# Two heads' attention worked as a pair, with query-key products alternating between the row halves of TensorE

## The chip, the cores and the metric

The kernel runs on one core of one Trainium2 chip. The core has a matrix engine (TensorE: PE in the profile, its weight loads PEld), a vector engine (VectorE, DVE), a scalar engine (ScalarE, ACT), GpSimd (POOL) and an engine that issues transfers (SyncE, SP). Each works off its own queue in order. TensorE writes to PSUM, from where VectorE and ScalarE fetch its results. The metric is the device time of one execution in microseconds, less being better.

## The reference

A two-layer encoder runs over two sequences that share their weights, one of 512 and one of 256 tokens, with a model width of 1024. The change is in the mixer of the first layer, which has eight attention heads of width 64 beside a short gated convolution:

```python
def window_conv_mixer(xn, pos, w_in, w_out, conv_w):
    z = xn @ w_in
    q, k, v, bg, cg, h = jnp.split(z, cuts, axis=-1)
    q = partial_rotary(heads(q), pos) * (HEAD_DIM ** -0.5)
    k = partial_rotary(heads(k), pos)
    ya = dilated_attention(q, k, heads(v)).reshape(B, S, A_WIDTH)
    yb = short_gated_conv(bg, cg, h, conv_w)
    return jnp.concatenate([ya, yb], axis=-1) @ w_out
```

`dilated_attention` runs three banded branches (window 128, 512 and 2048 with dilation 1, 4 and 16) and mixes them by the softmax of their log-sums. That equals one softmax over all keys in which each key's exponential is weighted by the number of branches that see it, and this is what the kernel computes. Behind the mixer come, in both layers, a cross-attention to 256 memory tokens and a SwiGLU; the second layer's mixer is an RWKV-7 recurrence.

## The kernel before

Activations lie with channels on partitions and tokens in columns, T = 768 columns for both sequences (`SEQS` cuts them at 512). A dense product is made from float32r pieces: each operand is cut into a high and a low part, and three matmuls (high by high, high by low, low by high) stand for one float32 product. `mms` (lines 342 to 344) does this for dense products: 8 blocks of 128 channels, for each block three matmuls with 512 columns and three with 256, 24 of each per output block of 128 channels. `products` (line 333) does the same for the attention.

In the first layer's mixer a pair p of heads shares one block of 128 channels: head 0 on partitions 0 to 63, head 1 on 64 to 127. There are four pairs. `keys(p)` and `values(p)` make q, k and v of a pair, `turned` transposes v, `conv(p)` makes the convolution's output of a block, `out(p)` adds the pair's share of the output product to the residual (line 755). `attend(p)` does the attention of a pair: for head 1 and then head 0, for each sequence, for each tile of 128 queries, it makes the three query-key products into a PSUM tile "sm" (a 64-row product: the contraction is over one head's 64 channels), adds the mask and takes the maximum (line 716, VectorE), exponentiates (718, ScalarE), weights by the count and sums (720), inverts the sum (722) and scales (723). The tile before it is then handed to `turn`: transposes by TensorE into another "sm" tile (693), a copy of the high part by ScalarE (695), the low part by VectorE (696), and after every second tile the products with v into `py` (line 333 again). Head 1's probabilities are multiplied with both heads' columns of v, and head 0's products then overwrite its half.

In PSUM "sm" has two buffers of 512 columns, "mm" for the dense products two of 768, `py` one. "e", the exponentials' tile, has three buffers. `bigs` holds the other work tiles.

The order of issue is set in two steps. `weave` interleaves generators: at each step it advances the one that is least far along relative to the number given with it. The order in which instructions are written becomes their priority. A planner then lays the instructions out on a simulated clock (the kernel asks for it with `schedule_with_timeline_sim=True`): an engine that is free takes the instruction of highest priority among those whose operands and buffers are ready. The resulting order of each engine is fixed, and on the chip each queue waits at its head. In the kernel before, the four pairs' attention is one generator of 52 steps, woven with one chain of dense work of 70 and the normalisation of the memory tokens of 32:

```python
weave((attends(), 52), (itertools.chain(*dense), 70), (mem_norm, 32, 12))
weave((part(out, 3), 4))
```

`dense` is the list of convolutions, keys, values and outputs in the order in which they are needed, with the memory's keys and values for the first cross-attention (`mem_kv`, `mem`) as its last members, some of them ahead of out(2). In the second layer, line 1179 (`inverse` in `mixer1_scan`) makes products with 64 rows whose loop alternates between the halves of the array; its operands are plain float32.

Of the kernel before, what the change touches and what calls it, by code (L numbers as in the profile page):

```python
# [9 lines left out]
F32 = mybir.dt.float32  # L10
# [27 lines left out]
class Net:  # L38
# [85 lines left out]
    def consts(self):  # L124
        nc, a = self.nc, self.a
        self.ident = self.cst.tile([128, 128], F32, name="ident")
        make_identity(nc, self.ident)
        self.ones = self.cst.tile([128, 128], F32, name="ones")
        nc.vector.memset(self.ones, 1.0)
        self.col = param_columns()  # L130
        n = sum(VECTORS.values())
        self.par = self.cst.tile([128, n], F32, name="par")
        nc.sync.dma_start(self.par, a["par"])
        self.mu = self.cst.tile([128, 2, 48], F32, name="mu")
        m = self.par[:, self.col["rw_mu"]:self.col["rw_mu"] + 48]
        nc.gpsimd.tensor_scalar(self.mu[:, 0], m, -1.0, 1.0, op0=OP.mult, op1=OP.add)
        nc.gpsimd.tensor_scalar(self.mu[:, 1], m, 0.5, None, op0=OP.mult)

        self.gmu = self.cst.tile([128, 2, 48], F32, name="gmu")
        c = self.col["norm_mix"] + KT  # L140
        nc.gpsimd.tensor_mul(self.gmu.rearrange("p a (i m) -> p (a i) m", m=KT), self.mu.rearrange("p a (i m) -> p (a i) m", m=KT),
                             self.par[:, c:c + KT].unsqueeze(1).to_broadcast([128, 12, KT]))
# [61 lines left out]
    def rstd(self, acc, spread=True):  # L204
# [4 lines left out]
        for t in range(n):  # L209
            for i, s in enumerate(acc):  # L210
                nc.tensor.matmul(ps[:, t:t + 1], lhsT=s[:, t * 128:(t + 1) * 128], rhs=self.ones[:, 0:1],  # L211
# [410 lines left out]
    def mixer0(self):  # L622
# [62 lines left out]
        def attend(p, o):  # L685
            q, k = o["q"], o["k"]
            py = self.pmm.tile([128, T], F32, name="py", bufs=1)

            def turn(e, pT, hs, s0, t, n):

                p2 = self.psm.tile([128, 4, 128], F32, name="sm")
                for i in range(n // 128):
                    nc.tensor.transpose(p2[:, i, :], e[:, i * 128:(i + 1) * 128], self.ident)
                hi, lo = cut(pT, slice(0, n // 128), slice(t % 2 * 128, t % 2 * 128 + 128))
                nc.scalar.copy(hi, p2[:, :n // 128])
                nc.vector.tensor_sub(lo, p2[:, :n // 128], hi.bitcast(F32))
                if t % 2:
                    c = s0 + t * 128 - 128

                    vs = slice(0, hs.stop)  # L700
                    self.products(py[vs, c:c + 256], [(cut(o["V"], s0 // 128 + i, vs), cut(pT, i)) for i in range(n // 128)])
            todo = None
            for h in (1, 0):
                hs = slice(64 * h, 64 * h + 64)
                for s0, s1 in SEQS:
                    n = s1 - s0
                    for t in range(n // 128):
                        if t % 2 == 0:
                            pT = [self.ph.tile([128, 4, 256], F32R, name="pT" + s, bufs=1) for s in "hl"]
                        off = 384 - 128 * t  # L710
                        ps = self.psm.tile([128, 512], F32, name="sm")
                        c = s0 + t * 128
                        self.products(ps[:, :n], [([a[hs, c:c + 128] for a in q], [a[hs, s0:s1] for a in k])])
                        e = self.at(512).big("e")
                        mx = self.tp.tile([128, 1], F32, name="mx0")
                        nc.vector.tensor_tensor_reduce(e[:, :n], ps[:, :n], self.mask[:, off:off + n], -1.0, 3e38,
                                                       OP.add, OP.min, mx)
                        nc.scalar.activation(e[:, :n], e[:, :n], AF.Exp, bias=mx, scale=-1.0)
                        den = self.tp.tile([128, 1], F32, name="den0")
                        nc.vector.tensor_tensor_reduce(e[:, :n], e[:, :n], self.cnt[:, off:off + n], 1.0, 0.0,  # L720
                                                       OP.mult, OP.add, den)
                        nc.vector.reciprocal(den, den)
                        nc.vector.tensor_scalar_mul(e[:, :n], e[:, :n], den)
                        if todo:
                            turn(*todo)
                        todo = e, pT, hs, s0, t, n
                        yield
            turn(*todo)
            o["ya"] = self.split(py, tag="y", bufs=6)
            yield  # L730

        def conv(p, o):
# [12 lines left out]
            o["yb"] = self.split(h, tag="y", bufs=6)  # L745
            yield

        def out(p, o):
            wa = self.wcols(w_out, p * 128, 1, 0, D)
            wb = self.wcols(w_out, 512 + p * 128, 1, 0, D)  # L750
            for m in range(KT):
# [4 lines left out]
                if m % 2:  # L756
# [6 lines left out]
        dense = [two(conv, 0), two(keys, 1), two(values, 1), two(conv, 1), two(keys, 2), part(out, 0), two(conv, 2),  # L763
                 two(values, 2), two(keys, 3), two(conv, 3), part(out, 1), two(values, 3), take(mem, 12), part(out, 2), mem]
# [5 lines left out]
        def attends():  # L770
            for p in range(4):
                turned(st[p])
                yield from attend(p, st[p])
        weave((attends(), 52), (itertools.chain(*dense), 70), (mem_norm, 32, 12))
# [267 lines left out]
    def mixer1_scan(self, L, rkv, zs, bvs, fill):  # L1042
# [33 lines left out]
        def prep(u, o):  # L1076
# [80 lines left out]
            for p, c in parts:  # L1157
                rk = self.tp.tile([128, 128], F32, name="rk")
# [459 lines left out]
```

## Time and profile before

| | us |
|---|---|
| median of three runs | 3124.48 |
| lowest, highest | 3120.39, 3129.13 |
| the profiled execution | 3129.72 |
| its span, first to last instruction | 3127.9 |
| TensorE busy in it | 2967.1 |
| VectorE busy in it | 1863.9 |

Times are compared by medians; durations and spans come from the one profiled execution. A row of the profile names the line, the engine, the operation, the tile written and those read ("sm<-qk"), the shape, and how often it stands (x3). For a matmul the shape is rows by output partitions of the array, then partitions by columns. A matmul's duration reaches from its start to its modelled end, and matmuls overlap in the pipeline. The first-layer attention lies between about 60 and 450 us; the mixer's last addition to the residual, by out(3), ends at about 485 us.

### The profile page before, as it was taken

Reading aid. Unit: us, or ns where it says so; the run is one execution under the profiler, and the core shown is the slowest. Engines: PE = TensorE matmul, PEld = TensorE weight load, DVE = VectorE, ACT = ScalarE, POOL = GpSimd, SP = SyncE. Lnnn points to the kernel's source line nnn. Section 1 sums busy time; section 2 is a strip of 40 time slices with the busy share of each in tenths; the row PEclk is TensorE's granted clock in tenths of the full one; section 3 lists DMA queues with packets and bytes.
Section 4 is the critical chain, followed back from the end, with each engine's and each line's share of the span. In section 5 each row is a group of like instructions: output and inputs, shape, how many; then the busy total and the mean of one; then the engine's idle time right before and its main releaser. Section 6 shows DMA issues by size and latency. Waiting matters only on the chain. (4 is left out here: it accounts for less than half of the span.)

```text
span 3127.9 us, 50086 instructions
## 1 busy us (share of the span) xinstructions
PE 2967.1 (95%) x19984; PEld 2465.7 (79%) x19984; DVE 1863.9 (60%) x3492; ACT 1223.7 (39%) x2241; POOL 608.6 (19%) x617
## 2 busy tenths in 40 slices
PE   7999999999999989889989999999999999999997
PEld 6888788888888867768767776666678888888886
DVE  8687547464354595376788777676636464334345
ACT  3232435332222375454546664554445232112112
POOL 3113004020000110122244223433335120000001
PEclk9999999999999999988979997999999999999998
DMA  3123332112355657644434552222352212212211
GB/s 116 48 68 115 105 118 85 58 54 68 119 192 193 218 173 261 203 155 144 142 104 146 165 158 75 71 71 66 117 166 79 71 41 68 68 54 68 68 55 54
DMA packets 349257, 344.15 MB, mean 110 GB/s; under 512 B 40928, under 2 KB 287840, under 8 KB 349024
## 3 DMA queue, kind: packets, MB, share of 16 engines
q1 hardware_dynamic: 349024, 340.96, 33.7%
q8 instruction: 157, 2.57, 0.3%
q14 instruction: 76, 0.62, 0.1%
HBM read 269.06 MB, written 71.83 MB: 109 GB/s over the span
## 5 line engine op out<-in xcount | busy, mean ns | idle before, releaser
L342 PE MATMUL mm<-xs,whi 128*128 128x512 f32 x2128 | 754.7, 356 | 32.0 <-ACT whi L274 11.8
L343 PE MATMUL mm<-xs,whi 128*128 128x512 f32 x2128 | 756.1, 355 | 3.1 <-DVE xs L237 2.2
L344 PE MATMUL mm<-xs,wlo 128*128 128x512 f32 x2128 | 750.4, 353 | 2.1 <-DVE wlo L275 2.1
L274 ACT CAST whi<-wraw 128x1024 fp32r<-128x1024 f32 (+1 forms) x246 | 256.3, 1044 | 789.1 <-PE mm L343 755.8
L342 PEld LDWEIGHTS mm<-xs,whi 128*128 128x128 f32 x2128 | 404.7, 190 | 95.6 <-ACT whi L274 12.4
L343 PEld LDWEIGHTS mm<-xs,whi 128*128 128x128 f32 x2128 | 404.6, 190 | 60.8 <-issue 3.3
L344 PEld LDWEIGHTS mm<-xs,wlo 128*128 128x128 f32 x2128 | 403.5, 190 | 60.7 <-DVE wlo L275 3.7
L275 DVE TENSOR_TENSOR wlo<-wraw,whi 128x1024 fp32r<-128x1024 f32 (+1 forms) x246 | 310.0, 1262 | 157.2 <-ACT whi L274 148.1
L201 POOL TENSOR_TENSOR acc<-acc,sq 128x768 f32<-128x768 f32 (+2 forms) x72 | 121.2, 1683 | 1417.3 <-ACT sq L198 1032.8
L343 PE MATMUL mm<-fb,thi 128*128 128x256 f32 (+1 forms) x720 | 236.3, 328 | 0.0
L342 PE MATMUL mm<-hid,whi 128*128 128x512 f32 (+1 forms) x528 | 186.5, 356 | 1.9 <-ACT hid L233 1.9
L343 PE MATMUL mm<-hid,whi 128*128 128x512 f32 (+1 forms) x528 | 187.8, 356 | 0.0
L344 PE MATMUL mm<-hid,wlo 128*128 128x512 f32 (+1 forms) x528 | 186.4, 354 | 0.0
L342 PE MATMUL mm<-fb,thi 128*128 128x256 f32 x528 | 170.3, 323 | 7.0 <-ACT thi L303 5.1
L303 ACT CAST thi<-traw 128x512 fp32r<-128x512 f32 (+1 forms) x202 | 122.6, 608 | 123.6 <-PE mm L343 72.0
L344 PE MATMUL mm<-fb,tlo 128*128 128x256 f32 x528 | 157.9, 301 | 10.2 <-DMA tlo<-low 5.2
L383 DVE SCALAR_TENSOR_TENSOR u<-mm,rstd 128x768 f32<-128x768 f32 (+1 forms) x44 | 38.4, 873 | 211.3 <-PE mm L344 211.3
L343 PEld LDWEIGHTS mm<-fb,thi 128*128 128x128 f32 x720 | 147.2, 204 | 5.1 <-issue 1.2
L403 DVE TENSOR_TENSOR x<-x,mm 128x512 f32<-128x512 f32 (+2 forms) x56 | 42.4, 762 | 175.3 <-PE mm L344 175.1
L1206 DVE TENSOR_TENSOR lt<-xr,lane 128x30 f32<-128x30 f32 (+4 forms) x360 | 130.4, 362 | 8.4
L342 PE MATMUL mm<-fa,thi 128*128 128x512 f32 (+1 forms) x304 | 132.5, 437 | 0.2 <-DVE fa L448 0.2
L1207 DVE TENSOR_TENSOR xr<-xr,lt 128x30 f32<-128x30 f32 (+4 forms) x360 | 124.7, 346 | 8.4
(366 smaller groups left out, 5906.2 us busy)
## 6 DMA issues: line engine op xcount, KB each, us to landing
wraw<-in_ffn_wgu_dram SPq DMA_DIRECT2D x44, 1024.0 KB, 4.9
tlo<-low SPq DMA_DIRECT2D x128, 256.0 KB, 3.2
low<-wlo SPq DMA_DIRECT2D x60, 512.0 KB, 3.1
wraw<-in_ffn_wdown_dram SPq DMA_DIRECT2D x23, 1024.0 KB, 4.9
traw<-in_ffn_wgu_dram SPq DMA_DIRECT2D x56, 256.0 KB, 3.8
wraw<-in_ab_w_in_dram SPq DMA_DIRECT2D x24, 512.0 KB, 3.6
wraw<-in_ca_wkv_dram SPq DMA_DIRECT2D x8, 1024.0 KB, 5.5
kvd<-kv SPq DMA_DIRECT2D x32, 256.0 KB, 2.0
```

Of the source, the lines that this page charges most:

```text
L201: nc.gpsimd.tensor_add(acc, acc, sq)
L274: nc.scalar.copy(hi[:, :, :m], raw[:, :, j:j + m])
L275: nc.vector.tensor_sub(lo[:, :, :m], raw[:, :, j:j + m], hi[:, :, :m].bitcast(F32))
L303: nc.scalar.copy(hi[:, :n], raw[:, :n])
L342: nc.tensor.matmul(ps[:, s0:s1], lhsT=wh, rhs=xh[:, s0:s1], start=start and k == 0, stop=False)
L343: nc.tensor.matmul(ps[:, s0:s1], lhsT=wh, rhs=xl[:, s0:s1], start=False, stop=False)
L344: nc.tensor.matmul(ps[:, s0:s1], lhsT=wl, rhs=xh[:, s0:s1], start=False, stop=stop and k == n - 1)
L383: nc.vector.scalar_tensor_tensor(u, pu, 0.5, rstd, op0=OP.mult, op1=OP.mult)
L403: self.nc.vector.tensor_add(self.x[m], self.x[m], ps)
L1206: nc.vector.tensor_mul(t, xr[:, m:, k:k + 1].to_broadcast([128, n, k]), ln[:, k:k + 1, 0:k].to_broadcast([128, n, k]))
L1207: nc.vector.tensor_add(xr[:, m:, 0:k], xr[:, m:, 0:k], t)
```

## The change

`attend` loops over sequences and query tiles once and treats both heads in each turn. The six query-key products of a pair of tiles are written so that heads alternate: pass one of head 0 and of head 1, pass two of both, pass three of both. Each head has its own "sm" tile, so both buffers are taken. Reductions and exponentials of both follow, and between them the transposes of the previous pair's tiles, first head 0's, then head 1's; the products with v of both heads follow head 1's transposes. Sum, inverse and scaling stand in a second step, the inverse for both heads in one instruction. The transposed probabilities need two sets of tiles.

The one chain of dense work becomes a list for each pair of heads, and each pair's attention is woven with its own list. The memory's keys and values stand at the end of the last list. "y", the tiles of split results that out(p) reads, goes from six buffers to four; `ones` shrinks to one column; `rk` of the second layer moves to another pool.

```diff
-        self.ones = self.cst.tile([128, 128], F32, name="ones")
+        self.ones = self.cst.tile([128, 1], F32, name="ones")
...
+            heads = [slice(0, 64), slice(64, 128)]
+            passes = ((0, 0), (0, 1), (1, 0))
-            def turn(e, pT, hs, s0, t, n):
+            def turn(h, es, pT, s0, t, n):
+                m = n // 128
                 p2 = self.psm.tile([128, 4, 128], F32, name="sm")
...
-                if t % 2:
+                if h and t % 2:
                     c = s0 + t * 128 - 128
-                    vs = slice(0, hs.stop)
-                    self.products(py[vs, c:c + 256], [(cut(o["V"], s0 // 128 + i, vs), cut(pT, i)) for i in range(n // 128)])
+                    for vs, pt in ((slice(0, 128), pT[1]), (slice(0, 64), pT[0])):
+                        self.products(py[vs, c:c + 256], [(cut(o["V"], s0 // 128 + i, vs), cut(pt, i)) for i in range(m)])
             todo = None
-            for h in (1, 0):
-                hs = slice(64 * h, 64 * h + 64)
-                for s0, s1 in SEQS:
-                    n = s1 - s0
-                    for t in range(n // 128):
-                        if t % 2 == 0:
-                            pT = [self.ph.tile([128, 4, 256], F32R, name="pT" + s, bufs=1) for s in "hl"]
-                        off = 384 - 128 * t
-                        ps = self.psm.tile([128, 512], F32, name="sm")
-                        c = s0 + t * 128
-                        self.products(ps[:, :n], [([a[hs, c:c + 128] for a in q], [a[hs, s0:s1] for a in k])])
...
-                        if todo:
-                            turn(*todo)
-                        todo = e, pT, hs, s0, t, n
-                        yield
-            turn(*todo)
-            o["ya"] = self.split(py, tag="y", bufs=6)
+            for s0, s1 in SEQS:
+                n = s1 - s0
+                for t in range(n // 128):
+                    if t % 2 == 0:
+                        pT = [[self.ph.tile([128, 4, 256], F32R, name=f"pT{h}" + s, bufs=1) for s in "hl"] for h in range(2)]
+                    off = 384 - 128 * t
+                    ps = [self.psm.tile([128, 512], F32, name="sm") for _ in heads]
+                    c = s0 + t * 128
+                    for j, (u, v) in enumerate(passes):
+                        for h, hs in enumerate(heads):
+                            nc.tensor.matmul(ps[h][:, :n], lhsT=q[u][hs, c:c + 128], rhs=k[v][hs, s0:s1], start=j == 0, stop=j == 2)
+                    es, mx = [], self.tp.tile([128, 2], F32, name="mx0")
+                    for h in range(2):
+                        e = self.at(512).big("e")
+                        es.append(e)
+                        nc.vector.tensor_tensor_reduce(e[:, :n], ps[h][:, :n], self.mask[:, off:off + n], -1.0, 3e38,
+                                                       OP.add, OP.min, mx[:, h:h + 1])
+                        nc.scalar.activation(e[:, :n], e[:, :n], AF.Exp, bias=mx[:, h:h + 1], scale=-1.0)
+                        if todo:
+                            turn(h, *todo)
+                    yield
+                    den = self.tp.tile([128, 2], F32, name="den0")
+                    for h, e in enumerate(es):
+                        nc.vector.tensor_tensor_reduce(e[:, :n], e[:, :n], self.cnt[:, off:off + n], 1.0, 0.0,
+                                                       OP.mult, OP.add, den[:, h:h + 1])
+                    nc.vector.reciprocal(den, den)
+                    for h, e in enumerate(es):
+                        nc.vector.tensor_scalar_mul(e[:, :n], e[:, :n], den[:, h:h + 1])
+                    todo = es, pT, s0, t, n
+                    yield
+            for h in range(2):
+                turn(h, *todo)
+            o["ya"] = self.split(py, tag="y", bufs=4)
...
-        dense = [two(conv, 0), two(keys, 1), two(values, 1), two(conv, 1), two(keys, 2), part(out, 0), two(conv, 2),
-                 two(values, 2), two(keys, 3), two(conv, 3), part(out, 1), two(values, 3), take(mem, 12), part(out, 2), mem]
+        dense = [[two(conv, 0), two(keys, 1), two(values, 1)],
+                 [two(keys, 2), part(out, 0), two(conv, 1), two(values, 2)],
+                 [two(keys, 3), part(out, 1), two(conv, 2), two(values, 3)],
+                 [part(out, 2), two(conv, 3), mem]]
...
-        def attends():
-            for p in range(4):
-                turned(st[p])
-                yield from attend(p, st[p])
-        weave((attends(), 52), (itertools.chain(*dense), 70), (mem_norm, 32, 12))
+        for p, ds in enumerate(dense):
+            turned(st[p])
+            weave((attend(p, st[p]), 13), (itertools.chain(*ds), 4 * len(ds)), *[(take(mem_norm, 5), 12, 3)] * (p in (1, 2)))
         weave((part(out, 3), 4))
...
-                rk = self.tp.tile([128, 128], F32, name="rk")
+                rk = ph.tile([128, 128], F32, name="rk", bufs=2)
```

## Rows read from the trace of the kernel before

**Rows 1.** The page: busy us (share) xinstructions; busy tenths in 40 slices.
```profile
PE 2967.1 (95%) x19984; PEld 2465.7 (79%) x19984; DVE 1863.9 (60%) x3492; ACT 1223.7 (39%) x2241; POOL 608.6 (19%) x617
...
PE   7999999999999989889989999999999999999997
```

**Rows 2.** Windows: length, busy PE, PEld, DVE, ACT, POOL, PEclk, DMA share, GB/s.
```profile
60.00:450.00 390.00, 389.19 (x2159) 322.89 (x2158) 269.69 (x518) 128.10 (x192) 51.29 (x35) 1.00 0.26 84
160.00:180.00 20.00, 20.00 (x105) 15.85 (x105) 19.96 (x36) 6.05 (x8) 7.19 (x6) 1.00 0.19 54
450.00:520.00 70.00, 69.97 (x400) 60.94 (x399) 39.87 (x52) 32.52 (x48) 25.66 (x12) 1.00 0.36 121
```

**Rows 3.** Waits of TensorE from 60 to 450 us: total us, times, longest.
```profile
PE mm L342 <- ACT xs L236: 0.5, 1, 0.5
PE sm L333 <- DVE mx L716: 0.3, 1, 0.3
```

**Rows 4.** Timeline of TensorE around a 512-key product group: start us, us, what.
```profile
162.54 0.29 PE L343 MATMUL mm<-xs,whi 128*128 128x256 f32 x1
162.66 0.28 PE L344 MATMUL mm<-xs,wlo 128*128 128x256 f32 x1
162.87 0.96 PE L333 MATMUL sm<-qk 64*128 64x512 f32 x3
163.76 0.51 PE L342 MATMUL mm<-xs,whi 128*128 128x512 f32 x1
164.11 0.40 PE L343 MATMUL mm<-xs,whi 128*128 128x512 f32 x1
164.34 0.40 PE L344 MATMUL mm<-xs,wlo 128*128 128x512 f32 x1
```

**Rows 5.** Timeline of TensorE around a 256-key product group.
```profile
96.92 0.60 PE L693 MATMUL sm<-ident,e 128*128 128x128 f32 x4
97.45 0.61 PE L333 MATMUL sm<-qk 64*128 64x256 f32 x3
98.00 0.39 PE L343 MATMUL mm<-xs,whi 128*128 128x256 f32 x1
98.22 0.28 PE L344 MATMUL mm<-xs,wlo 128*128 128x256 f32 x1
```

**Rows 6.** Timeline of TensorE: two groups in direct succession.
```profile
66.50 1.65 PE L333 MATMUL sm<-qk 64*128 64x512 f32 x6
```

**Rows 7.** Timeline of TensorE, second layer: line 1179, two visits.
```profile
1660.80 1.16 PE L1179 MATMUL g<-ar,bk 64*128 64x128 f32 x8
1661.88 0.50 PE L1026 MATMUL e<-blk,kksq 128*128 128x2 f32 x3
...
1734.44 1.16 PE L1179 MATMUL g<-ar,bk 64*128 64x128 f32 x16
1735.53 0.39 PE L344 MATMUL mm<-fb,tlo 128*128 128x256 f32 x1
```

**Rows 8.** Lines, 60 to 450 us: busy us, mean ns, idle before.
```profile
L275 DVE TENSOR_TENSOR wlo<-wraw,whi 128x1024 fp32r<-128x1024 f32 x40 | 51.7, 1294 | 14.7 <-ACT whi L274 9.8 <-PE sm L490 4.8
...
L333 PE MATMUL sm<-qk 64*128 64x512 f32 (+1 forms) x144 | 40.9, 389 | 0.3 <-DVE mx L716 0.3
...
L716 DVE CUSTOM_DVE_ANT_0 e<-sm,mask 128x512 f32<-128x512 f32 (+1 forms) x48 | 28.7, 599 | 20.7 <-PE sm L333 20.6
L696 DVE TENSOR_TENSOR pTl<-sm,pTh 128x512 fp32r<-128x512 f32 (+1 forms) x48 | 28.6, 598 | 29.4 <-ACT pTh L695 29.2
...
L693 PE MATMUL sm<-ident,e 128*128 128x128 f32 x160 | 25.4, 273 | 0.0
L695 ACT CAST pTh<-sm 128x512 fp32r<-128x512 f32 (+1 forms) x48 | 24.6, 514 | 89.5 <-PE sm L693 82.4 <-PE py L333 7.0
...
L722 DVE RECIPROCAL den<-den 128x1 f32<-128x1 f32 x48 | 7.7, 161 | 0.9
L486 ACT COPY kv<-mm 128x512 f32<-128x512 f32 x13 | 7.6, 585 | 1.7 <-PE mm L344 1.7
```

More of the change, by code (lines that the diff above doesn't have):

```diff
@@ L210, in rstd @@
             for i, s in enumerate(acc):
-                nc.tensor.matmul(ps[:, t:t + 1], lhsT=s[:, t * 128:(t + 1) * 128], rhs=self.ones[:, 0:1],
+                nc.tensor.matmul(ps[:, t:t + 1], lhsT=s[:, t * 128:(t + 1) * 128], rhs=self.ones,
                                  start=i == 0, stop=i == len(acc) - 1)
@@ L687, in attend @@
             py = self.pmm.tile([128, T], F32, name="py", bufs=1)
-            def turn(e, pT, hs, s0, t, n):
+            heads = [slice(0, 64), slice(64, 128)]
+            passes = ((0, 0), (0, 1), (1, 0))
+            def turn(h, es, pT, s0, t, n):
+                m = n // 128
                 p2 = self.psm.tile([128, 4, 128], F32, name="sm")
[L692 to L696, printed above, removed]
-                if t % 2:
+                for i in range(m):
+                    nc.tensor.transpose(p2[:, i, :], es[h][:, i * 128:(i + 1) * 128], self.ident)
+                hi, lo = cut(pT[h], slice(0, m), slice(t % 2 * 128, t % 2 * 128 + 128))
+                nc.scalar.copy(hi, p2[:, :m])
+                nc.vector.tensor_sub(lo, p2[:, :m], hi.bitcast(F32))
+                if h and t % 2:
@@ L698, in turn @@
                     c = s0 + t * 128 - 128
-                    vs = slice(0, hs.stop)
-                    self.products(py[vs, c:c + 256], [(cut(o["V"], s0 // 128 + i, vs), cut(pT, i)) for i in range(n // 128)])
+                    for vs, pt in ((slice(0, 128), pT[1]), (slice(0, 64), pT[0])):
+                        self.products(py[vs, c:c + 256], [(cut(o["V"], s0 // 128 + i, vs), cut(pt, i)) for i in range(m)])
             todo = None
-            for h in (1, 0):
-                hs = slice(64 * h, 64 * h + 64)
-                for s0, s1 in SEQS:
-                    n = s1 - s0
-                    for t in range(n // 128):
-                        if t % 2 == 0:
-                            pT = [self.ph.tile([128, 4, 256], F32R, name="pT" + s, bufs=1) for s in "hl"]
-                        off = 384 - 128 * t
-                        ps = self.psm.tile([128, 512], F32, name="sm")
-                        c = s0 + t * 128
-                        self.products(ps[:, :n], [([a[hs, c:c + 128] for a in q], [a[hs, s0:s1] for a in k])])
-                        e = self.at(512).big("e")
[L715 to L719, printed above, removed]
-                        nc.vector.tensor_tensor_reduce(e[:, :n], e[:, :n], self.cnt[:, off:off + n], 1.0, 0.0,
-                                                       OP.mult, OP.add, den)
-                        nc.vector.reciprocal(den, den)
-                        nc.vector.tensor_scalar_mul(e[:, :n], e[:, :n], den)
-                        if todo:
-                            turn(*todo)
-                        todo = e, pT, hs, s0, t, n
-                        yield
@@ L744, in conv @@
             nc.vector.tensor_mul(h, h, yb)
-            o["yb"] = self.split(h, tag="y", bufs=6)
+            o["yb"] = self.split(h, tag="y", bufs=4)
             yield
```

## The prediction

> **What bounds the kernel now.** I began with the page: TensorE is busy for 95% of the span, in every slice for 7 tenths or more, VectorE for 60% [rows 1]. The changed code runs in the second to sixth slices, so I asked next for a window over that stretch. From 60 to 450 us TensorE is busy for 389.19 of 390.00 us at the full granted clock (1.00, the 2.4 GHz level), VectorE for 269.69 [rows 2]. The waits of TensorE in the same stretch come to 0.8 us in two pieces [rows 3]. So this stretch lasts as long as TensorE's own work in it, and a microsecond less of that work is a microsecond less of time, as long as no wait takes its place. Behind it, from 450 to 520 us, TensorE is busy for 69.97 of 70.00 us [rows 2]: what is won isn't given back at once to a late load.
>
> Busy time still hides something: how long a matmul occupies TensorE is the distance from its start to the next start, not its duration. That I read from the timeline. Dense matmuls with 512 columns start 0.23 us apart (164.11 to 164.34), those with 256 columns 0.12 us apart (162.54 to 162.66) [rows 4]. A group of three query-key products uses 64 rows of the array, and it costs more than three such steps. The row before it starts at 162.66, the next dense matmul after it at 163.76: 1.10 us, of which 0.12 belong to the dense one, so 0.98. The first dense matmul behind the group then takes 0.35 us to its successor instead of 0.23, another 0.12. Together 1.10 us, of which 3 x 0.23 = 0.70 are streaming and 0.40 is the price of going from 128 rows to 64 and back [rows 4]. With 256 keys the row before the group is one of four transposes, 0.60 us together and 0.27 each [rows 5, 8], so (0.60 - 0.27) / 3 = 0.11 apart and 0.44 for the four. Then 97.45 - 96.92 - 0.44 = 0.09 us pass on the way in, 98.00 - 97.45 = 0.55 for the group, and 98.22 - 98.00 - 0.12 = 0.10 behind it: 0.74 us, of which 3 x 0.12 = 0.36 are streaming [rows 5].
>
> **The change part by part.** *Pairs of heads.* There are 144 products [rows 8], 48 groups: 32 with 512 keys, 16 with 256. They take 32 x 1.10 + 16 x 0.74 = 47.0 us, of which 32 x 0.70 + 16 x 0.36 = 28.2 are streaming. Groups in direct succession share one switch (six products in 1.65 us of busy time); there are three such places, 3 x 0.40 = 1.2 us less: 45.8 us [rows 4 to 6].
>
> After the change there are 24 groups of six, alternating between the row halves. Before has no such pair in this number format, so the price has two ends. If the halves run one behind the other, only switches go: 45 become 24, (45 - 24) x 0.40 = 8.4 us. If they run together, a pair streams in the time of one: 16 x 1.10 + 8 x 0.74 = 23.5 us, plus a few hundredths for each pair's offset, call it 24.0, and the gain is 21.8 us. The nearest rows are those of line 1179 in the second layer, which alternates halves of 64 rows into two tiles in just this way, in plain float32. One visit has 16 records in 1.16 us of busy time, with 1.09 us to the next matmul; another has 8 records in the same 1.16 and 1.08 us [rows 7]. Twice the work in one time, weight loads included: the halves run together wherever the two are issued alternately. I take 21.8.
>
> The Trainium skill ("TensorE: Matmul & The Clock Gate", Part 3) gives a smaller yield of such packing: four row tiles with 512 columns reached 3.07 times the rate of one, 0.77 of what four could be. By that two halves give 1.53 times, the 28.2 us of streaming would shrink by 9.8 us instead of by half, and the gain would be about 18, an estimate from the page's figure. The visits above show 2.0, and the measurement goes first.
>
> *Who issues.* The same rows also hold a warning. The loop of line 1179 alternates, yet one of the visits has 8 records as slow as the other's 16. The planner takes any instruction that is ready, so when one head's "sm" buffer is free before the other's it issues that head's products alone. Query-key pairs take both "sm" buffers, and these come free at two times, after the two heads' evacuations. In the written order about one dense product, 24 matmuls or 8 x 3 x (0.23 + 0.12) = 8.4 us [rows 4], stands before each new pair. That is longer than the lag between the buffers: one transposition 0.60 [rows 5], one copy 0.51 and one subtraction 0.60 [rows 8], 1.7 us. So most pairs should find both buffers free. The ends are the whole gain and, with every pair split, none. I keep 0.85 of it, nearer to the whole for the reason just given: 18.5 us.
>
> *Two heads' softmax.* The same reductions, exponentials and scalings are issued; 48 reciprocals become 24, 24 x 0.161 = 3.9 us less on VectorE [rows 8], off the path. Transposes and probability-value products keep number and shape; they stand in larger clumps.
>
> *The dense list in four parts.* The same matmuls in another order. In before, 13 outputs of the memory keys and values fall into the 390 us [rows 8], each of 24 matmuls with 512 columns, 13 x 24 x 0.23 = 72 us of TensorE with only 13 x 1.29 = 17 us of weight splitting on VectorE. Now nearly all of that runs behind the last pair, and its cover for the fourth pair's attention goes. Attention and the rest must share about 389 - 72 - 22 = 295 us of TensorE with 270 - 17 - 4 = 249 us of VectorE: 84%, against 69% before. TensorE stays the longer, but the slack is halved. VectorE was full for 19.96 of 20 us from 160 to 180, and TensorE lost nothing there [rows 2]. That is the one end, 0; the other is the whole gain. The row is near, so I take 3 us.
>
> *Buffers.* "y" goes from 6 to 4, covered by the earlier out(p), which now stands ahead of the conv that writes next; without that cover a conv's split would wait out one out() of some 17 us, off TensorE's path as the next dense work is ready. The ones, the rk and the pT tiles move or resize storage and issue nothing new: I cost them at zero, as no wait of TensorE is for them [rows 3].
>
> *Sum.* 18.5 - 3 = 15.5 us. The profiled execution took 3129.72 us (span 3127.9 and 1.8 around it), 5.2 above the median of 3124.48; in its terms 3114, from the median 3109.
>
> **The rivals.**
> *Split pairs.* The planner issues most pairs head by head. For it: the slow visit of line 1179 [rows 7]. Against it: the 8.4 us of dense work per pair. At half the pairs or fewer alternated the gain is 11 us less 3, so 3116.
> *VectorE takes over the pace.* At 84% on average it is over 90% somewhere, and its dense evacuations queue behind softmax. Half to all of the gain turns into waits of TensorE: 3113 to 3124, say 3119. Against it: the stretch from 160 to 180 us [rows 2]. The Trainium skill ("TensorEngine Tiling (Array Packing)", PSUM Bottleneck) names this: tiling speeds up TensorE but not the evacuation of PSUM. The trace of before can't show it for these pairs.
> *Slower: the pair's chain sets the pace.* Two "sm" buffers and three "e" buffers serve a pair, so a new pair follows only when product 1.1, reduction 0.60, transposition 0.60, second reduction 0.60, second transposition 0.60, copy 0.51 and subtraction 0.60 us have followed each other, 4.6 us without hand-overs [rows 4, 5, 8]. A dense operation of 1.29 us on VectorE [rows 8] in front of each of the three VectorE steps makes 8.5, and hand-overs come on top. A pair's share of TensorE is 295 / 24 = 12.3 us. Above that TensorE waits, and since its queue runs in order, the dense matmuls written behind the waiting product wait with it; from 0.9 us of wait per pair the gain is gone (22 / 24), from 1.3 us the change is slower by the bound below. At 2 us it costs 48 - 22 = 26: 3150; at 1.3, 3134. For it: dense work that ends early leaves nothing to hide under.
> *No overlap in this format.* The gain is 8.4 less 3: 3119. Against it: the two visits [rows 7].
>
> **How the numbers follow.** A measurement of this kernel tells about 0.3% from no change, 9.4 us: faster is below 3115, slower above 3134. Chances: the forecast (gain of 10 to 24 us, 3100 to 3114) 0.57; split pairs 0.13; VectorE's pace 0.13; slower 0.12; no overlap 0.05. Of the three middle cases about 0.04 still falls below 3115. So faster 0.61, same 0.27, slower 0.12. The range runs from the full gain with 2 or 3 us of luck, 3100, to 3126, which takes in the middle cases and leaves out the slower one and a little at the foot. The forecast's own range is 3100 to 3114.
>
> **What the changed profile would show.** Groups of six query-key products between dense matmuls, two starts within hundredths of a microsecond, about 1.1 us for 512 keys and 0.75 for 256 from dense to dense. If products stand in threes, the planner split them. TensorE's waits from 60 us to the end of the stage should stay under about 5 us; waits of dense products on z or of transposes on e would be VectorE's pace or the chain. The last addition of out(3) should come some 15 us earlier than before, and the span behind it stay as long. The prediction is wrong if that later span changes, or if TensorE's waits reach 0.9 us per pair.

## The result and the profile after

Over five runs each, the changed kernel takes 3152.88 us (3137.61 to 3157.68) against 3121.61 (3120.39 to 3129.13) before: a ratio of 1.0085, 95% interval 1.0056 to 1.0114. It is slower by some 27 us in the mean, where 15 less were forecast. The profiled execution took 3146.99 us against 3129.72, 17.3 more, and is the basis of what follows.

The page of the changed kernel, busy time and TensorE's slices:

```profile
PE 2971.3 (94%) x19984; PEld 2469.7 (79%) x19984; DVE 1854.8 (59%) x3468; ACT 1224.1 (39%) x2241; POOL 606.8 (19%) x617
...
PE   7999999999999989889989998999999999999997
```

VectorE has the 24 reciprocals less, and TensorE's instructions are as many as before [rows 1]; its busy time went up by 4 us although less was to be streamed. The windows say where (length, busy PE, PEld, DVE, ACT, POOL, PEclk, DMA share, GB/s):

```profile
60.00:450.00 390.00, 380.36 (x2089) 315.99 (x2089) 261.44 (x492) 123.05 (x184) 52.02 (x36) 0.98 0.26 80
450.00:520.00 70.00, 67.47 (x362) 57.55 (x360) 32.62 (x26) 32.76 (x45) 25.59 (x12) 1.00 0.35 113
...
142.60:146.00 3.40, 3.40 (x17) 3.00 (x15) 3.10 (x4) 0.16 (x1) 1.86 (x2) 0.50 0.67 213
...
149.40:152.80 3.40, 3.40 (x11) 2.78 (x10) 1.63 (x5) 1.35 (x2) 2.41 (x3) 0.51 0.62 158
```

In the attention's stretch TensorE is idle for 9.64 us where it was idle for 0.81 [rows 2], and the granted clock is no longer 1.00 throughout. Five pieces at the 1.2 GHz level, 17.1 us together, lie at 143, 149, 245, 320 and 385 us, where before had none. (A sixth lies ahead of them, at 40 us; before has one like it at 22 us.) TensorE's waits from 40 to 520 us (total us, times, longest), against 1.4 us in the same stretch before, of which [rows 3] hold 0.8:

```profile
PE sm L717 <- DVE Vl L683: 2.9, 3, 2.2
PE mm L342 <- ACT whi L274: 2.5, 1, 2.5
PE py L333 <- ACT pT1h L698: 2.2, 2, 1.1
PE sm L680 <- DVE pT0l L699: 2.2, 2, 1.6
PE mm L342 <- ACT y L233: 0.8, 1, 0.8
PE py L333 <- DVE pT1l L699: 0.7, 1, 0.7
```

These and three more of 0.2 to 0.6 us make 12.6. Line 717 is now the query-key product, 680 the transposition of v at a pair's start, 698 and 699 the copy and the subtraction of the transposed probabilities. Of the 12.6 us, 8.2 lie at the three seams between pairs of heads, that is, at the last products of one pair and the first transposes and products of the next. Another 1.5 us come near the end of the last pair, the 2.5 behind out(3), and the rest at the stage's start, as before. The timeline of TensorE across the first seam (start us, us, what, idle before and its releaser):

```profile
145.17 0.84 PE L680 MATMUL sm<-ident,z 128*128 128x128 f32 x3
148.21 0.96 PE L717 MATMUL sm<-qk 64*128 64x512 f32 x3 [2.20 <-DVE Vl L683]
149.10 0.95 PE L342 MATMUL mm<-y,whi 128*128 128x512 f32 x2
149.85 0.63 PE L343 MATMUL mm<-y,whi 128*128 128x512 f32 x1
150.28 0.63 PE L344 MATMUL mm<-y,wlo 128*128 128x512 f32 x1
150.71 0.41 PE L342 MATMUL mm<-y,whi 128*128 128x256 f32 x1
```

Three things stand here. TensorE has no dense matmul left while v goes through copy and subtraction, and idles 2.20 us. The dense work behind it is out(0) (it reads "y", the result of the attention that has just ended). keys(2), which stand ahead of it in the list, had been worked by then (VectorE ends their rotation at 145.81), and the planner drew nothing from behind out(0) ahead of it. And then the clock is down: 512-column matmuls start 0.43 us apart (149.85 to 150.28) instead of 0.23 [rows 4]. At the same seam of the kernel before, dense products of the layer's input ("xs") run up to the transposes and on behind them, without a wait:

```profile
148.46 0.28 PE L344 MATMUL mm<-xs,wlo 128*128 128x256 f32 x1
148.58 0.38 PE L693 MATMUL sm<-ident,e 128*128 128x128 f32 x2
148.79 0.49 PE L680 MATMUL sm<-ident,z 128*128 128x128 f32 x3
149.04 0.48 PE L342 MATMUL mm<-xs,whi 128*128 128x512 f32 x1
```

The groups of query-key products, from two places of the changed kernel's timeline:

```profile
72.57 0.39 PE L342 MATMUL mm<-xs,whi 128*128 128x512 f32 x1
72.89 0.97 PE L717 MATMUL sm<-qk 64*128 64x512 f32 x6
73.79 0.50 PE L343 MATMUL mm<-xs,whi 128*128 128x512 f32 x1
...
85.50 0.39 PE L344 MATMUL mm<-xs,wlo 128*128 128x512 f32 x1
85.82 0.96 PE L717 MATMUL sm<-qk 64*128 64x512 f32 x3
86.71 0.39 PE L342 MATMUL mm<-xs,whi 128*128 128x256 f32 x1
```

Six products of a pair take 0.90 us from their start to the next dense matmul, three of one head 0.89: the second head is free. Six of one half took 1.57 us to the next dense matmul (from 66.50 to 68.07 in the trace of before), with 1.65 us of busy time [rows 6]. But the six are rare. Of the 45 groups of query-key products 42 hold three products ("threes") and 3 hold six ("sixes"), and of the sixes one is three and three with a wait between, one overlaps only in part.

Out(3)'s last addition to the residual ends at 501.7 us instead of 485.6, 16.1 later; the span behind it is 2643.5 us against 2642.3, 1.2 longer. So in the profiled executions the loss is made in the stage that was changed.

### The profile page after: what moved, and what is told of

Its sections match the earlier page's. It is cut to its first block, busy times and chain, and to the rows that moved or that the text cites. A ratio compares the mean times of both kernels' runs of the same rounds, so it can differ in the third digit from the quotient of the medians.

```text
span 3145.2 us, 50096 instructions
## 1 busy us (share of the span) xinstructions
PE 2971.3 (94%) x19984; PEld 2469.7 (79%) x19984; DVE 1854.8 (59%) x3468; ACT 1224.1 (39%) x2241; POOL 606.8 (19%) x617
## 5 line engine op out<-in xcount | busy, mean ns | idle before, releaser
L344 PE MATMUL mm<-fb,tlo 128*128 128x256 f32 x528 | 157.4, 300 | 11.5 <-DMA tlo<-low 7.9
```

The costliest lines, as they stand in the source:

```text
L344: nc.tensor.matmul(ps[:, s0:s1], lhsT=wl, rhs=xh[:, s0:s1], start=False, stop=stop and k == n - 1)
```

## The experiments

All ratios are to the kernel before, in the same session, with 95% intervals. As a second measure I give the end of out(3)'s last addition in the profiled execution (485.6 before, 501.7 changed).

**The lists alone.** The attention of before, head after head; only the four lists of dense work and their weaving are the change's:

```diff
-        dense = [two(conv, 0), two(keys, 1), two(values, 1), two(conv, 1), two(keys, 2), part(out, 0), two(conv, 2),
-                 two(values, 2), two(keys, 3), two(conv, 3), part(out, 1), two(values, 3), take(mem, 12), part(out, 2), mem]
+        dense = [[two(conv, 0), two(keys, 1), two(values, 1)],
+                 [two(keys, 2), part(out, 0), two(conv, 1), two(values, 2)],
+                 [two(keys, 3), part(out, 1), two(conv, 2), two(values, 3)],
+                 [part(out, 2), two(conv, 3), mem]]
...
-        weave((attends(), 52), (itertools.chain(*dense), 70), (mem_norm, 32, 12))
+        for p, ds in enumerate(dense):
+            turned(st[p])
+            weave((attend(p, st[p]), 13), (itertools.chain(*ds), 4 * len(ds)), *[(take(mem_norm, 5), 12, 3)] * (p in (1, 2)))
```

> The kernel before with one part of the change alone: the dense chain cut into one list for each pair of heads, each woven with its pair's attention; the attention itself stays head by head. Theory 1 (the lists cost the time: at a pair's end the list holds little but out(p), which needs that very end, and TensorE stands still): waits of TensorE of 2 us and more at each of the first three pair ends, and drops of its granted clock there as in the changed kernel; the last addition of out(3) 10 to 18 us later than before, the time 3132 to 3145. Theory 2 (the paired attention costs the time, by its buffers): no new waits, 3118 to 3126.

Measured 3152.47 us, 1.0083 (1.0058 to 1.0109); out(3) ends at 497.1. TensorE's longest waits, 40 to 520 us:

```profile
PE mm L342 <- ACT whi L274: 2.6, 1, 2.6
PE sm L333 <- DVE Vl L683: 2.2, 2, 1.5
PE mm L342 <- DVE x L755: 1.9, 1, 1.9
PE py L333 <- ACT pTh L695: 1.3, 3, 0.6
```

The waits stand at the same seams, smaller than expected, without any pair of heads, and the time is above the range that I gave. Over the whole kernel the lists alone cost what the whole change costs. In this profile 11.5 us stand at out(3); by the last addition of the first cross-attention it is 16 (569 to 553), where the changed kernel has 19. The rest of this execution's loss, some 8 us, comes in the second layer's recurrence, which no line of the edit touches. I can't account for it; the clock there differs from one profiled execution to the next. Between 840 and 2340 us the half level holds some 222 us here, 215 before, 205 in the changed kernel, and over the kernels below 191 to 246. Such a difference is worth up to half its length, so out(3) is the steadier measure.

**One tile for a pair.** The changed kernel, with both heads' products in one tile of two banks, so that they can't come apart. There is then one such buffer, and the transposes of the pair before are written ahead of the products:

```diff
-        self.nmm = 2
+        self.nmm, self.nsm = 2, 1
...
-        self.psm = pool("psm", 2)
+        self.psm = pool("psm", self.nsm)
...
-                    ps = [self.psm.tile([128, 512], F32, name="sm") for _ in heads]
+                    if todo:
+                        turn(*todo)
+                    both = self.psm.tile([128, 2, 512], F32, name="sm")
+                    ps = [both[:, h] for h in range(2)]
```

> The changed kernel, but the two heads' products go to one tile of two banks with a single buffer, so that the planner can't take one head's products without the other's; the transposes of a pair share such a tile too and are written ahead of the next pair's products. Theory 1 (pairs run together wherever they are issued together, and the changed kernel's were issued in threes): 24 groups of six, about 0.9 us from the first product to the next dense matmul with 512 keys and 0.55 with 256, which is 20 to 22 us less of TensorE's work than in the changed kernel; the waits at the pair ends stay, so 3125 to 3138 against 3153 for the changed kernel. Rival (no overlap in float32r): 1.6 and 0.9 us for a group, 3143 to 3150. Second rival (one buffer makes the chain of a pair longer than TensorE's work beside it): waits of products on VectorE at every pair, no gain over the changed kernel.

Measured 3224.08 us, 1.0316 (1.0289 to 1.0343); out(3) ends at 570.4. All 24 groups are sixes. Where nothing interrupts them they take 0.89 to 0.91 us with 512 keys, 0.55 with 256, as priced. But TensorE waits:

```profile
PE sm L697 <- DVE e L736: 36.6, 9, 8.9
PE sm L697 <- DVE pT0l L700: 16.7, 12, 3.4
PE sm L721 <- DVE pT1l L700: 6.8, 5, 2.2
```

Line 697 is the transposition, 736 the scaling of the exponentials, 700 the subtraction that frees the buffer. With one buffer the pair's whole softmax lies between its products and its transposes, and TensorE runs into it.

**The convolution first.** The changed kernel with two members exchanged in three of the lists, so that out(p), which needs the attention that has just ended, doesn't stand first:

```diff
-                 [two(keys, 2), part(out, 0), two(conv, 1), two(values, 2)],
-                 [two(keys, 3), part(out, 1), two(conv, 2), two(values, 3)],
-                 [part(out, 2), two(conv, 3), mem]]
+                 [two(keys, 2), two(conv, 1), part(out, 0), two(values, 2)],
+                 [two(keys, 3), two(conv, 2), part(out, 1), two(values, 3)],
+                 [two(conv, 3), part(out, 2), mem]]
```

> The changed kernel with one thing moved: in the lists of the last three pairs the convolution stands ahead of out(p) instead of behind it, so that at a pair's end products are left that don't need its result. Theory 1 (the lists' order makes TensorE wait at the pair ends): the waits there vanish, with the drops of the granted clock; 3128 to 3140, about the kernel before plus what little the three paired groups save. Rival (the waits come from the paired attention's own buffers): the waits stay and the time stays at 3147 to 3158.

Measured 3127.35 us, 1.0004 (0.9989 to 1.0020); out(3) ends at 481.9. Windows and TensorE's waits from 40 to 520 us:

```profile
60.00:160.00 100.00, 100.00 (x584) 83.32 (x583) 79.52 (x143) 32.47 (x50) 25.68 (x17) 1.00 0.21 61
160.00:260.00 100.00, 99.66 (x578) 83.22 (x577) 74.47 (x141) 29.87 (x45) 25.59 (x18) 1.00 0.31 96
```
```profile
PE mm L342 <- ACT whi L274: 2.5, 1, 2.5
PE mm L342 <- DVE x L765: 0.8, 2, 0.5
PE mm L342 <- DVE z L643: 0.6, 1, 0.6
```

One exchange takes the whole loss back; the four lists stay, so it isn't the cutting that costs but what stands where. The waits at the seams are gone, and with them the half clock: the first such piece is at 483 us. VectorE has as much to do as in the changed kernel, so its load was not the cause. Four groups are sixes, three of them with both heads side by side from the start; out(3) is 3.7 us earlier than before, about what they are worth at 1.1 us each. This doesn't reach the end: behind out(3) the first weight of the cross-attention is cast late (the 2.5 us), which all kernels with the four lists show and before doesn't.

**Both.** The single tile together with the convolution first, the two diffs above in one.

> Both together: one tile for a pair, and the convolution ahead of out(p). If the two causes are the whole of it and add up, TensorE's work falls by about 20 us and no wait takes its place: 3100 to 3112, faster than the kernel before. If the pair's chain through a single buffer sets the pace, 3115 to 3135 with waits of products or transposes at each pair.

Measured 3225.57 us, 1.0325 (1.0298 to 1.0351), far outside both ranges given. The order of the lists makes no difference that shows once the pair's chain sets the pace.

**Pairs held together, two buffers.** The convolution first, and all six products also wait for both subtractions that free the two "sm" buffers:

```diff
-                nc.vector.tensor_sub(lo, p2[:, :m], hi.bitcast(F32))
+                o["freed"].append(nc.vector.tensor_sub(lo, p2[:, :m], hi.bitcast(F32)))
...
+                    for a in made:
+                        for b in o["freed"]:
+                            self.tc.add_manual_dep(a.ins, b.ins.name, mybir.DependencyInfo(mybir.DependencyClass.Sync, mybir.DependencyReason.DATA), reason="pair")
+                    o["freed"] = []
```

> The changed kernel with the convolution ahead of out(p), as in the run where that was moved alone, and one thing more: all six products of a pair also wait for both subtractions that free the two buffers, so the planner has no reason to take one head's products first. Both buffers stay separate and the transposes keep their place. In the planned order 22 pairs stand in six and two are split. Theory (split pairs were all that kept the gain away once the lists are mended): about 20 pairs more than in that run go together, 16 of 512 keys at 1.10 and 8 of 256 at 0.74 us saved in all, so 18 to 20 us less, 3103 to 3112 against the kernel before's 3127. Rival (a pair that waits for both buffers starts later, and its chain then sets the pace): new waits of TensorE on VectorE or ScalarE in most pairs and drops of its clock, no gain or a loss, 3120 to 3180.

Measured 3151.72 us, 1.0075 (1.0053 to 1.0096); out(3) ends at 509.5. 22 groups are sixes. The pairs follow each other at 92.5, 111.0, 127.9 and 145.3 us, so 17 to 18 us apart. VectorE's timeline through one of them, between products at 92.54 and 110.95:

```profile
94.32 0.68 DVE L727 CUSTOM_DVE_ANT_0 e<-sm,mask 128x512 f32<-128x512 f32 x1
...
98.15 0.69 DVE L727 CUSTOM_DVE_ANT_0 e<-sm,mask 128x512 f32<-128x512 f32 x1 [1.54 <-PE sm L696]
...
99.37 0.95 DVE L643 SCALAR_TENSOR_TENSOR z<-mm,rstd 128x768 f32<-128x768 f32 x1
100.24 1.22 DVE L275 TENSOR_TENSOR wlo<-wraw,whi 128x1024 fp32r<-128x1024 f32 x1
...
102.90 2.65 DVE L655 TENSOR_TENSOR r<-r,rot 128x512 f32<-128x512 f32 x2
...
105.55 0.67 DVE L699 TENSOR_TENSOR pT1l<-sm,pT1h 128x512 fp32r<-128x512 f32 x1
```

The reductions (line 727) are at 94.32 and 98.15, the subtraction that frees the second buffer at 105.55, although its copy stood at 102.79: in between VectorE evacuates, splits and rotates the dense work. The chain is 18.4 us where a pair's share of TensorE is 12.3 by the prediction's estimate. TensorE's waits come to 31 us from 40 to 520 us, and the clock spends 47.8 us at the half level before 600 us.

**Pairs held together, lists of the change.** The same waits, with out ahead of the convolution:

```diff
-                 [two(keys, 2), two(conv, 1), part(out, 0), two(values, 2)],
+                 [two(keys, 2), part(out, 0), two(conv, 1), two(values, 2)],
```

> The same added waits in the changed kernel as it is, with out(p) ahead of the convolution: 24 groups of six. If the two causes add up, it is 18 to 21 us faster than the changed kernel and still pays for its pair ends: 3128 to 3138. If waiting for both buffers lengthens the chain, the waits at the pair ends grow and the time is that of the changed kernel, 3150, or more.

Measured 3167.01 us, 1.0130 (1.0096 to 1.0164); out(3) ends at 517.3, with 24 sixes. Chain and seams together cost more than each.

**A third buffer.** The convolution first, and a third "sm" buffer. The bank for it comes from `py`, which now holds one sequence at a time; the stage's first product, which lay there, takes two "sm" tiles instead:

```diff
-            py = self.pmm.tile([128, T], F32, name="py", bufs=1)
+            ya, acc = self.pair("y", 4), {}
...
+                    if c == 0:
+                        acc[s0] = self.pmm.tile([128, 512], F32, name="py", bufs=1)[:, :n]
...
-        early[1024] = product(1024, "py", bufs=1)
+        early[1024] = [self.psm.tile([128, 512], F32, name="sm") for _ in SEQS]
```

> The changed kernel with the convolution ahead of out(p) and a third buffer for the tile sm: the products with v go to a tile of one sequence instead of both, which frees a bank, and the first value product of the stage goes to two sm tiles in place of that tile. No wait is added. In the planned order 12 of the 24 pairs stand in six. If pairing costs its gain only because two heads take both buffers, this keeps TensorE's waits as low as with the convolution moved alone, and 8 more pairs together save 6 to 8 us more: 3112 to 3122 against 3127 for the kernel before. If the three e tiles or VectorE's queue hold the pairs up, waits return and it is 3127 or more.

Measured 3124.46 us, 0.9996 (0.9982 to 1.0011). 13 groups are sixes instead of 4, but out(3) ends at 482.6, no earlier, and the gain that I expected didn't come. The stage's start shows why, in the windows and TensorE's waits up to 62 us:

```profile
40.00:60.00 20.00, 12.90 (x65) 11.24 (x65) 17.55 (x38) 1.69 (x3) 7.01 (x5) 0.74 0.18 52
```
```profile
PE sm L186 <- DVE bc L180: 7.1, 1, 7.1
```

Before, TensorE was busy for 19.44 of these 20 us at the full clock. The product that now takes both "sm" tiles holds up the statistics that need one, and the clock falls: 10.2 us of it at half.

**A third buffer, pairs held together.** The six products also wait for the two reductions of the pair before and for the one subtraction that frees the third buffer:

```diff
-                nc.vector.tensor_sub(lo, p2[:, :m], hi.bitcast(F32))
+                sub = nc.vector.tensor_sub(lo, p2[:, :m], hi.bitcast(F32))
+                if h == 0:
+                    o["freed"].append(sub)
...
+                        o["freed"].append(r)
```

> The same with three buffers, and the six products of a pair also wait for both reductions of the previous pair and the subtraction that frees the third buffer; in the planned order 19 pairs stand in six. If two buffers were all that made a waiting pair late, the pairs follow each other in 12 us or less and the time falls by 15 to 18 us against the kernel with the convolution moved: 3106 to 3116. If the chain is long because its VectorE steps queue behind dense work, pairs follow each other in 14 us or more, the waits and the clock's drops return, and the time is 3130 to 3160.

Measured 3115.84 us, 0.9964 (0.9950 to 0.9978); 20 groups are sixes, out(3) ends at 474.0. The loss of 7.1 us at the start is still in it.

**The start covered.** The same, with the first product's 512 columns in the free `py` and only its 256 in an "sm" tile:

```diff
-        early[1024] = [self.psm.tile([128, 512], F32, name="sm") for _ in SEQS]
+        early[1024] = [self.pmm.tile([128, 512], F32, name="py", bufs=1), self.psm.tile([128, 512], F32, name="sm")]
```

> The kernel with three buffers and waiting pairs, and the start of the stage mended: its first value product goes to the free py tile (512 columns) and one sm tile (256), instead of two sm tiles, which had made it wait behind the norm's tiles and left TensorE idle for 7.1 us with its clock halved from 42 to 52 us. If that start is all that the three-buffer kernel loses against its own gain in the attention, the idle piece and the low clock go and the time falls by 7 to 12 us against it: 3104 to 3111, with the last addition of out(3) near 463 us. If the planner's order of the whole stage shifts instead, 3111 to 3120.

Measured 3113.42 us, 0.9941 (0.9913 to 0.9968), faster than the kernel before; out(3) ends at 468.9, 5.1 us earlier than without the cover. The time is above the range given for the cover alone, and its interval overlaps with the one without the cover. Windows and waits, the latter from 40 to 520 us:

```profile
40.00:60.00 20.00, 20.00 (x109) 17.23 (x109) 18.11 (x40) 2.75 (x4) 6.27 (x5) 0.91 0.28 79
```
```profile
60.00:160.00 100.00, 100.00 (x611) 84.33 (x610) 81.73 (x160) 36.52 (x57) 24.16 (x17) 1.00 0.20 61
160.00:260.00 100.00, 97.79 (x595) 83.50 (x594) 79.66 (x153) 30.96 (x49) 27.28 (x19) 0.98 0.30 91
```
```profile
PE mm L347 <- DVE x L788: 2.8, 2, 2.2
PE mm L347 <- ACT whi L274: 2.5, 1, 2.5
```

The start is full again, VectorE at 79 to 82% leaves TensorE three waits of 5.3 us in all, and out(3) is 16.7 us earlier than before. 19 groups are sixes and one more is a six with a record missing. By the prediction's price, 20 of 24 pairs are 21.8 x 20 / 24 = 18.2 us, and the piece at half clock at 180 us takes up to 1.7 of them.

**Head after head, in one clump.** The last kernel with the loops exchanged, so that head 0's three products are followed by head 1's three:

```diff
-                    for j, (u, v) in enumerate(passes):
-                        for h, hs in enumerate(heads):
+                    for h, hs in enumerate(heads):
+                        for j, (u, v) in enumerate(passes):
```

> The same kernel with only the order of the two loops over passes and heads exchanged: the three products of head 0 and then the three of head 1, with the same buffers, waits and switches. If overlap of the row halves is worth what the prediction took, 16 pairs of 512 keys lose up to 0.70 us each and 8 of 256 up to 0.36, less one step at the seam: 9 to 14 us slower than the alternating one, 3115 to 3124. If alternation is worth nothing, both times are equal within 3 us.

Measured 3117.48 us, 0.9957 (0.9936 to 0.9978); out(3) ends at 466.1. The intervals of the two overlap widely: no difference was found, and the loss of 9 to 14 us for products that don't alternate didn't come. 20 of its groups are sixes of the same length; out(3) is 19.5 us earlier than before, where the price gives 18.2. The timeline of TensorE:

```profile
66.65 0.40 PE L348 MATMUL mm<-xs,whi 128*128 128x512 f32 x1
66.98 0.98 PE L735 MATMUL sm<-qk 64*128 64x512 f32 x6
67.89 0.50 PE L349 MATMUL mm<-xs,wlo 128*128 128x512 f32 x1
```

Six products in 0.91 us, though TensorE's queue holds them as three of one tile and then three of the other. What pays is that both heads' products stand together, not that they alternate.

Not tried: paired attention with the one chain of dense work of before.

## Why the prediction was wrong, step by step

**What bounds the stage** was right: the loss is in the stage, TensorE's time sets it, and the later span is the same within 1.2 us. That this is so close is in part luck: it holds some 10 us less at half clock than before (205 against 215 between 840 and 2340 us).

**The price of a pair** was right. Six take 0.90 and 0.55 us, as three do [rows 4, 5], and the 21.8 us for 24 pairs fit the last two kernels: 16.7 and 19.5 us at out(3) with 20 pairs together, for which the price gives 18.2. The smaller yield of the Trainium skill ("TensorE: Matmul & The Clock Gate", Part 3), 3.07 of 4, doesn't show here: two halves gave 2.0, as in [rows 7]. "No overlap in this format" falls with it.

**"Who issues"** is the first step that failed. I kept 0.85 of the gain since 8.4 us of dense work stand before each pair in the written order. But the written order is only a priority: the first buffer that comes free lets one head's three products go, and the other's follow behind dense matmuls. The share was one pair in 24 and part of another in the changed kernel, worth some 1.8 us (1.1 for the one; the other takes 1.29 us and the 0.21 us around it [rows 4] where two threes take 2.20). With the convolution first it was three and a part. This is the rival "Split pairs", at a smaller share than it was priced for. That the buffers are the cause is shown by the runs: a third buffer alone brings 13 sixes, waits on both buffers 22.

**"The dense list in four parts"** is the step that turned the sign. I took 3 us for it, between none and the whole gain, and weighed it by VectorE's load, with the stretch from 160 to 180 us as the nearest row [rows 2]. It cost some 17 us at out(3), near the upper of these ends but for another reason: 12.6 - 2.5 - 1.4 = 8.7 us of waits more than before (the 2.5 for a weight come behind out(3)), and up to half of the 17.1 us at half clock, 8.5. The exchange in the lists gave 501.7 - 481.9 = 19.8 us back, some 2 of them by more pairs. VectorE's load was not the cause: it was 261.44 of 390 us against 269.69 before, and 262.77 with the convolution first, where the waits are gone. The 84% didn't come either: VectorE is busy for 218.28 of the first 295 us of the stretch, 74%, and 10 of the 13 outputs of the memory keys and values still fall into the 390 us. What decided was which dense work is left when a pair of heads ends: in the lists of the change only out(p), which reads that pair's own result. In before's chain products that don't need it stood there, at the first seam the end of a convolution and the next keys. And the clock had no term in the sum at all. "VectorE takes over the pace" is refuted as a cause, too: at 79 to 82% of VectorE the kernel with the covered start waits only 2.8 us, for the residual.

**The sum** in measured terms: -1.8 for the pairs, 8.7 for waits and 8.5 for the clock are 15.4 us at out(3), where 16.1 were measured; with 1.2 behind it the profiled execution is 17.3 us longer than that of before (3146.99 to 3129.72). The means of the five runs are 26.6 us apart: the profiled execution of before took longer than all five of its own, that of the change less than the median of its own. The remaining 9 us are in no trace, and where they arise is not shown.

**"Slower: the pair's chain sets the pace"** is not what made the changed kernel slow; its pairs were split, and a split pair doesn't wait for both buffers. It is what happens when pairs are held together with two buffers: 17 to 18 us from pair to pair against the limit of 12.3 given there, and 24 us lost at out(3). The Trainium skill ("TensorEngine Tiling (Array Packing)", Gotcha 1: PSUM Pressure) says that row tiling raises the pressure on PSUM, as its tiles write to different banks. The runs agree: waits that hold pairs together make the kernel 0.75% slower than before with two buffers and 0.36% faster with three, though what they wait for differs too.

**Buffers, the ones, `rk` and the reciprocals** cost nothing, as said: the kernel with the convolution first has all of them and the time of before. But the order that was to cover for the fewer "y" tiles, out(p) ahead of the convolution, is the one that cost the time; without it no wait for them shows.

**What the profile would show**: sixes and waits under 5 us were named for success, threes for the planner's splitting. Threes came, and waits of more than 5 us. The two signs named for a wrong prediction did not come: the later span is the same, and 8.7 us of waits are 0.36 us for each of 24 pairs, not 0.9. They stand together at few places, and the clock fell behind them.

## What to carry to other kernels

When a list of work that hides something is cut into pieces, look at what is left at each cut: the work that stands there must not need what has just ended. Instructions that pay only together must be held together by what they wait for, with enough buffers that the wait costs nothing; written order is not enough where a planner reorders. A gain of 0.6% was in this change, but it needed four things beside it: the order at the seams, waits that hold a pair together, a third buffer and its cover at the start.

## What the hardware showed that I had not expected

Products on the two row halves ran side by side even when they stood in the queue as three and three (0.90 to 0.91 us for six, against 0.89 to 0.91 alternating; 0.56 against 0.55 with 256 keys). The Trainium skill ("TensorE: Matmul & The Clock Gate", Part 3) has matmuls start strictly in program order; by that the second three would begin no earlier than the last of the first three, and the six would take about 1.4 us, an estimate from 0.89 us for three and two steps of 0.23. The run doesn't bear this out. Which record belongs to which head the trace doesn't tell, so how it comes about stays open.

Waits of 0.2 to 2.2 us of TensorE, at the three seams and near the last pair's end, were followed by pieces at the 1.2 GHz level (143, 149, 245, 320, 385 us) that cost up to nearly as much again as the waits (8.5 us beside 8.7). With the waits gone, in the kernel with the convolution first, these pieces are gone too. In the kernel with pairs held together over two buffers, 47.8 us ran at that level before 600 us, against 3.4 before.
